# A later offer for the products of a recurrence: one constant in a planner that orders a whole kernel

## The chip, the core and the metric

The kernel runs on one core of a Trainium2 chip. The core has a matrix engine (TensorE, PE in the profile, with its weight loads shown apart as PEld), three engines for element work (VectorE or DVE, ScalarE or ACT, GpSimd or POOL), an engine that issues most transfers (SyncE, SP), and 16 DMA engines. Each engine works off its own queue in order. The metric is the device time of one launch in microseconds; less is better.

## The reference

One layer of a streaming encoder trunk works on 2048 prompt frames and 32 sample frames of width 1024. One input projection feeds two branches; branch A is attention in a band of chunks, branch B a gated delta rule with 8 heads of 64 in chunks of 64 frames. Both are gated, projected, merged, projected once more, added to the residual and normalised. The change lies in the delta rule's scan over the chunks:

```
def block(s, z):              # s: state (heads, 64, 64), one step per chunk
    r  = v  - k_decayed @ s           # what the state already explains
    vn = solve(r)                     # the chunk's triangular system
    o  = q_decayed @ s + qk @ vn      # the chunk's output
    s  = decay * s + k_rest.T @ vn    # the state for the next chunk
    return s, o
```

Each step needs the one before: three products and three element steps follow one another for 16 chunks per half of the prompt, for each pair of heads.

## The kernel before

The program is written by generators (streams) which a planner, `Flow`, resumes from a heap in the order of a modelled clock. What a stream emits between two yields is appended to the engines' queues, so the planner's clock sets the order in which each engine gets its work; on the chip nothing but queue order and data then decides when it runs. A bare `yield` puts the stream back at its own clock, plus `HOP_SAME` = 0.12 us if its last instruction was VectorE's; that addition moves only the key in the heap. A yielded float raises the stream's clock itself. `spend` books an instruction: it starts at the stream's clock plus a hop (`HOP_PE` = 0.1 for TensorE when the stream's last instruction was on another engine, `HOP` = 0.2 for the others) or when the modelled engine is free.

All engine instructions are recorded by one helper, so they carry line 267 in the profile (268 after the change, which adds a line above), and transfers carry 290 or 301.

The stages: the prompt is handled in two halves. In each, the input projection (`multiply`, tile `pj`, one matmul per yield, 512 or 272 columns wide, `hi`/`lo` and `whi`/`wlo` being the two parts of the split operands) runs beside the preparation and the recurrence of the delta rule (phase B, the recurrence at about 190 to 450 us and 910 to 1240 us) and then beside attention (phase A). In the second half's phase A the gated outputs of finished blocks already go through the branch projections (`early`, tiles `b<-ghi,whi`, `b<-glo,whi`), from about 1300 us on. The merge follows, from about 1709 us: for each block of 256 frames the merged activations (`mh`, their low part `ml`; `ms` for the sample rows) are multiplied with the output weights (`wohi`, `wolo`, `woh`, `wol`) into PSUM banks `a`, `a`, `a`, `c`, or by turns `pj`, `pj`, `b`, `b` once the early branch products are over. `finish` adds the result to the residual row `xt` (scaled before by rows `l0g`, `l0b` on GpSimd and VectorE), normalises and stores it.

The recurrence is `chain`, shown below. Tile names: `x` holds its three products (`x<-state,k_bd`, `x<-r,u_bd`, `x<-vn,kd_bd`), `o` its outputs, `r`, `vn` and `state` are VectorE's results. Two chains are open at a time (two banks `x`), and each takes a block of 8 chunks for a pair of heads; with the sample block there are 132 steps in all, hence 396 places where a product of TensorE follows VectorE. A small stream, `outputs`, emits the products into `o`.

Of the kernel before, what the change touches and what calls it, by code (L numbers as in the profile page):

```python
# [58 lines left out]
ORDER += [(NP - 1, 3)]  # L59
MARGIN = 1.6  # L60
SLACK = 2.5
LEAD = 5.0
ZERO = 1.2
BLOCKS = [
# [211 lines left out]
def trunk(ctx: ExitStack, tc: tile.TileContext, x_p, x_s, cache_k, cache_v, st_conv, st_gdn,  # L276
# [4 lines left out]
    flow = Flow()  # L281
# [6 lines left out]
    def dma(dst, src, eng=nc.sync):  # L288

        eng.dma_start(dst, src)  # L290
        size = 2 if dst.dtype == F16 else 4
        n = size
        for k in dst.shape:
            n *= k

        n = max(n, n // (size * dst.shape[-1]) * 768)
        return flow.transfer("SP" if eng is nc.sync else "S", n)

    def turn(dst, src):
# [5 lines left out]
        flow.busy["SP"] = max(flow.busy.get("SP", 0.0), flow.cur.clock + 0.2) + 0.8  # L305
        return flow.transfer("SP", n * 1.5) + SLACK

# [338 lines left out]
    def load_rows(w, k, to, ready):  # L646
# [4 lines left out]
        for c in range(2):  # L651
            hi, lo = to(c)
            flow.start(split(hi, lo, wr[:, c * 512:(c + 1) * 512], both[c], V if k % 2 else G, t + SLACK, ready(c)))
        yield
# [26 lines left out]
    def divide():  # L681

        while True:
# [7 lines left out]
            sc = w_scale[:, job.wid:job.wid + 1]  # L691
            yield t + (SLACK if len(started) > 4 else 0.0)
            started.append(job)
# [88 lines left out]
    def split(hi, lo, wr, give, eng, t, m):  # L782
        yield t
        S.copy(out=hi, in_=wr)
        yield
        eng.tensor_tensor(out=lo, in0=wr, in1=hi.bitcast(F32), op=ALU.subtract)
        if give:
            give()
        m.done()
# [50 lines left out]
    def phase_b(half):  # L840
# [535 lines left out]
        def outputs(m, x, os_, vc=None, end=None):  # L1376


            PE.matmul(os_, m, x, start=vc is None, stop=vc is not None)
            yield  # L1380
            if vc is not None:
                S.copy(out=vc, in_=os_)
                if end:
                    end.done()

        def chain(some):
            for k in some:
                yield k.ready
                xn = yield from x_banks.take()
                sc, v_t = k.sc, k.v_t  # L1390
                xs, ys, ds_ = (xb[xn][:, i * HD:(i + 1) * HD] for i in range(3))
                os_ = ob_[xn][:, 0:HD]
                for c in range(k.nch):
                    st = k.state[c]
                    vc = v_t[:, c if k.p is None else c % 4 * 2 + c // 4, :]
                    PE.matmul(xs, k.kb[:, c, :], st, start=True, stop=True)
                    yield
                    r = bp.tile([P, HD], F32, tag=f"r{xn}", bufs=2, name="r")
                    V.scalar_tensor_tensor(out=r[:], in0=xs, scalar=k.negc[:, c:c + 1], in1=vc, op0=ALU.mult, op1=ALU.add)
                    yield  # L1400
                    PE.matmul(ys, k.ub[:, c, :], r[:], start=True, stop=True)
                    flow.start(outputs(k.qb[:, c, :], st, os_))
                    yield
                    vn = bp.tile([P, HD], F32, tag=f"vn{xn}", bufs=2, name="vn")
                    V.tensor_scalar(out=vn[:], in0=ys, scalar1=sc[:, 1, c:c + 1], scalar2=None, op0=ALU.mult)
                    yield
                    PE.matmul(ds_, k.kdb[:, c, :], vn[:], start=True, stop=True)
                    flow.start(outputs(k.qkb[:, c, :], vn[:], os_, vc, k.out if c == k.nch - 1 else None))
                    V.scalar_tensor_tensor(out=st, in0=st, scalar=sc[:, 3, c:c + 1], in1=ds_, op0=ALU.mult, op1=ALU.add)
                    yield  # L1410
                yield k.out
                x_banks.back(xn)
                par_slots.back(k.par)
                side_slots.back(k.sn)
                u_slots.back(k.un)
                flow.start(tail(k))
# [87 lines left out]
        for some in blocks + ([[sample]] if last else []):  # L1504
            flow.start(chain(some))
# [3 lines left out]
    def phase_a(half):  # L1509
# [424 lines left out]
        def leave_pair(k, t, gt, place):  # L1934
# [4 lines left out]
            cs = slice(gt * P, (gt + 2) * P)  # L1939
            at = dma(ga[:].rearrange("p i n -> p (i n)"), za_dram[k.p][:, cs]) + SLACK  # L1940
            yield at - LEAD / 4
            yield bank["b"]
# [19 lines left out]
        def sample(k):  # L1962
# [12 lines left out]
            kc_t, vc_t = cached  # L1975
            yield at + SLACK
            yield bank["b"]
# [132 lines left out]
    def last_weights():  # L2110
# [6 lines left out]
        def load(k, c, half):  # L2117
            cs = slice(c * 512, (c + 1) * 512)
            t = dma(half, w_out[k * P:(k + 1) * P, cs])
            flow.start(split(wo[0][k][:, cs], wo[1][k][:, cs], half, None, V if k % 2 else G, t, w_ready["o", k, c]))  # L2120
            yield t - LEAD

        def row(name, src):
# [3 lines left out]
            if name[0:2] == "l0":  # L2127
                flow.start(scale(rowv[name][:], t, name == "l0b"))
            yield t - LEAD

        def scale(r, t, last):
            yield t
            S.activation(out=r, in_=r, func=AF.Copy, scale=ALPHA)
            if last:
                rows_ready.done()
# [90 lines left out]
    def early():  # L2226
        while True:
# [12 lines left out]
            for f in range(KD):  # L2240
# [12 lines left out]
                def evac(f=f, sg=sg, slots=slots, ps=ps, t=t, c0=c0, n=n, what=what, br=br):  # L2253
                    yield t + SLACK
                    V.scalar_tensor_tensor(out=sg[:, 0:n], in0=sg[:, 0:n], scalar=1.0, in1=ps[:, 0:n],
                                           op0=ALU.add, op1=ALU.mult)
                    bank["b"].give()
                    yield
                    at = dma(sig_dram[br][f][:, c0:c0 + n], sg[:, 0:n])
                    for b, _, _ in what:  # L2260
                        early_done[br, b, f].done()
                    yield at
                    slots.give()
# [278 lines left out]
```

## Time and profile before

| what | value |
|---|---|
| median of three runs | 1983.99 us |
| the runs | 1983.57, 1987.36, 1983.99 us |
| the profiled execution | 1980.36 us |
| its span in the profile | 1978.6 us |
| granted TensorE clock, mean over the span | 0.988 |
| TensorE busy | 1894.8 us, 14513 matmuls |
| VectorE busy | 1421.8 us, 4458 instructions |
| ScalarE busy | 993.2 us |
| GpSimd busy | 814.7 us |

The profile is one execution, with the begin and the duration of every instruction, and for the idle time of an engine the instruction that ended it. The group lines read: engine, operation, output tile and input tiles, shapes, count, then busy time in us, mean duration in ns, and the engine's idle time just before these instructions with what ended it. Timeline rows begin with the start and the duration in us, and have the idle time before them and its end in brackets.

### The profile page before, as it was taken

How to read it: one execution, taken by the hardware profiler on the slowest of the kernel's cores; microseconds unless marked ns; L12 is line 12 of the kernel's file. 1: busy time of each engine (PE TensorE's matmuls, PEld its weight loads, DVE VectorE, ACT ScalarE, POOL GpSimd, SP SyncE). 2: the span in 40 equal slices, each digit the busy share in tenths (PEclk: the TensorE clock that was granted, in tenths of full speed). 3: DMA queues.
4: the chain of work that ended last, by engine and by line, in shares of the span. 5: the costliest groups of instructions: out<-in, count | busy, mean ns of one | idle time of the engine just before them, and what ended most of it. 6: DMA issues, size and time to landing. Idle time of an engine off the chain costs nothing.

```text
span 1978.6 us, 41065 instructions
## 1 busy us (share of the span) xinstructions
PE 1894.8 (96%) x14513; PEld 1338.2 (68%) x14513; DVE 1421.8 (72%) x4458; ACT 993.2 (50%) x2022; POOL 814.7 (41%) x1139
## 2 busy tenths in 40 slices
PE   8999999999999999999999999999999999989996
PEld 5455666676455556666776777678877668878874
DVE  7779989873378768579989986356466665585886
ACT  6665545444586777664544533445355774310110
POOL 7344334433344444343333432423122331363695
PEclk9999999999999999999999999999999999999998
DMA  4224242333378786223142243578878798975542
GB/s 139 68 83 125 65 108 70 84 92 108 115 159 197 188 179 156 71 79 89 52 118 68 68 112 83 139 212 192 227 173 199 168 215 177 310 272 191 167 152 83
DMA packets 382806, 274.62 MB, mean 139 GB/s; under 512 B 248322, under 2 KB 319342, under 8 KB 382600
## 3 DMA queue, kind: packets, MB, share of 16 engines
q1 hardware_dynamic: 382600, 272.00, 51.3%
q8 instruction: 114, 1.87, 0.4%
q14 instruction: 92, 0.75, 0.1%
HBM read 157.15 MB, written 71.76 MB: 116 GB/s over the span
## 4 chain that ended last, share of the span: by engine, by line
PE 64%; DVE 20%; issue 5%; ACT 4%; DMA 4%; POOL 3%; SPq 1%; POOLq 0%; DVEq 0%; ACTq 0%
PE pj L267 34%; PE b L267 15%; PE a L267 7%; PE c L267 4%; PE x L267 3%; DVE acc L267 3%; DVE sys_t L267 2%; DVE sys_u L267 2%; PE o L267 2%; DVE kd_bd L267 1%; POOL wlo L267 1%; SPq L290 1%; DVE xt L267 1%; DVE q_bd L267 1%; DMA sf<-sig 1%
## 5 line engine op out<-in xcount | busy, mean ns | idle before, releaser
L267 PE MATMUL pj<-hi,whi 128*128 128x512 f16 (+2 forms) x1992 | 642.3, 338 | 11.2 <-DVE zb L267 3.2
L267 PE MATMUL pj<-hi,wlo 128*128 128x512 f16 (+2 forms) x1952 | 633.8, 338 | 0.6 <-POOL wlo L267 0.5
L267 PEld LDWEIGHTS <-whi 128*128 128x128 f16 x3984 | 407.8, 104 | 227.3 <-issue 8.6
L267 POOL TENSOR_TENSOR wlo<-wraw,whi 128x256 f16<-128x256 f32 (+1 forms) x392 | 280.6, 738 | 460.9 <-ACT whi L267 380.5
L267 PE MATMUL pj<-lo,whi 128*128 128x512 f16 (+2 forms) x1992 | 452.5, 338 | 0.0
L267 PEld LDWEIGHTS <-wlo 128*128 128x128 f16 x1952 | 204.3, 105 | 115.2 <-issue 11.9
L267 ACT ACTIVATE sb<-sb,mx,unit 128x640 f32<-128x640 f32 (+4 forms) x128 | 108.6, 849 | 101.4 <-DVE mx L267 96.3
L267 POOL TENSOR_TENSOR pu<-sb,pu 128x640 f16<-128x640 f32 (+2 forms) x64 | 82.3, 1285 | 178.3 <-ACT pu L267 145.4
L267 ACT ACTIVATE wraw<-wraw,w_scale 128x1024 f32<-128x1024 f32 (+1 forms) x98 | 111.4, 1137 | 78.3 <-DVE w_scale L267 75.8
L267 PE MATMUL b<-ghi,whi 128*128 128x256 f32 (+1 forms) x512 | 138.7, 303 | 3.6 <-DVE cr L267 1.1
L267 ACT CAST whi<-wraw 128x512 f16<-128x512 f32 (+2 forms) x212 | 128.2, 611 | 27.5 <-PE pj L267 24.6
L267 PE MATMUL b<-ghi,wlo 128*128 128x256 f32 (+1 forms) x512 | 129.5, 284 | 0.0
L267 DVE TENSOR_TENSOR sys_u<-sys_u,sys_t 128x60 f32<-128x60 f32 (+24 forms) x527 | 124.6, 242 | 5.7
L267 DVE SCALAR_TENSOR_TENSOR acc<-raw,cwT,acc 128x512 f32<-128x512 f32 x144 | 112.7, 782 | 7.9 <-ACT acc L267 6.5
L267 ACT CAST mh<-sf 128x256 fp32r<-128x256 f32 x64 | 25.7, 406 | 178.8 <-PE c L267 74.8
L267 DVE TENSOR_TENSOR sys_t<-sys_u,sys_p 128x60 f32<-128x60 f32 (+21 forms) x459 | 109.8, 242 | 5.5
L267 PEld LDWEIGHTS b<-ghi,whi 128*128 128x128 f32 x512 | 97.3, 190 | 9.7 <-ACT ghi L267 1.5
L267 ACT COPY v_t<-o 128x64 f32<-128x64 f32 x132 | 27.7, 210 | 143.2 <-PE o L267 106.7
L267 PEld LDWEIGHTS b<-ghi,wlo 128*128 128x128 f32 x512 | 97.5, 190 | 1.5
L267 DVE CUSTOM_DVE_ANT_0 sb<-a,bias 128x320 f32<-128x320 f32 (+5 forms) x136 | 66.2, 497 | 45.0 <-PE a L267 42.4
L267 POOL TENSOR_TENSOR w_scale<-w_scale,mhalf 128x1 f32<-128x1 f32 x49 | 32.2, 657 | 157.3 <-DVE w_scale L267 113.8
L267 ACT ACTIVATE sig<-pj,w_half 128x512 f32<-128x512 f32 (+2 forms) x84 | 49.3, 587 | 77.0 <-PE pj L267 71.6
(377 smaller groups left out, 4097.7 us busy)
## 6 DMA issues: line engine op xcount, KB each, us to landing
wraw<-in_w_in SPq DMA_DIRECT2D x192, 256.0 KB
sf<-sig SPq DMA_DIRECT2D x112, 128.0 KB
sig<-sig SPq DMA_DIRECT2D x44, 256.0 KB
sg<-sig SPq DMA_DIRECT2D x37, 256.0 KB
sig<-sg SPq DMA_DIRECT2D x37, 256.0 KB
sys_p<-sol_p SPq DMA_DIRECT2D x68, 128.0 KB
x<-in_x_p SPq DMA_DIRECT2D x16, 512.0 KB
xt<-in_x_p SPq DMA_DIRECT2D x16, 512.0 KB
```

What stands on the lines that cost most here:

```text
L267: r = f(*a, **k)
L290: eng.dma_start(dst, src)
```

## The change

Each of the chain's three yields that follow a VectorE instruction now yields a time instead of nothing: the stream's clock plus 0.15 us. Before, the stream came back at a key 0.12 us later with its clock unmoved; now key and clock are both 0.15 us later. The instructions themselves are the same.

```
+CHAIN = 0.15
...
                     V.scalar_tensor_tensor(out=r[:], in0=xs, scalar=k.negc[:, c:c + 1], in1=vc, op0=ALU.mult, op1=ALU.add)
-                    yield
+                    yield flow.cur.clock + CHAIN
                     PE.matmul(ys, k.ub[:, c, :], r[:], start=True, stop=True)
...
                     V.tensor_scalar(out=vn[:], in0=ys, scalar1=sc[:, 1, c:c + 1], scalar2=None, op0=ALU.mult)
-                    yield
+                    yield flow.cur.clock + CHAIN
                     PE.matmul(ds_, k.kdb[:, c, :], vn[:], start=True, stop=True)
...
                     V.scalar_tensor_tensor(out=st, in0=st, scalar=sc[:, 3, c:c + 1], in1=ds_, op0=ALU.mult, op1=ALU.add)
-                    yield
+                    yield flow.cur.clock + CHAIN
```

The order of all engines is the same up to the first steps of the first recurrence, and differs in many small pieces from there to the end. Three places follow.

TensorE in the first recurrence of half 0, before: `pj` are projection products, `b<-ident` transposes, the number behind a name tells tiles of one name apart.

```order
L267 MATMUL pj<-lo_163,whi 128x512
L267 MATMUL x<-vn,kd_bd_746 128x64
L267 LDWEIGHTS whi
L267 MATMUL pj<-lo_163,whi 128x512
L267 MATMUL o<-vn,qk_bd_739 128x64
L267 LDWEIGHTS whi
L267 MATMUL pj<-lo_163,whi 128x512
L267 MATMUL b<-ident,v_1845 128x128 x4
L267 LDWEIGHTS whi
L267 MATMUL pj<-lo_163,whi 128x512
L267 MATMUL x<-state,k_bd_735 128x64
```

The same place on TensorE after the change:

```order
L268 MATMUL pj<-lo_163,whi 128x512
L268 LDWEIGHTS whi
L268 MATMUL pj<-lo_163,whi 128x512
L268 MATMUL x<-vn,kd_bd_746 128x64
L268 MATMUL b<-ident,v_1845 128x128 x4
L268 LDWEIGHTS whi
L268 MATMUL pj<-lo_163,whi 128x512
L268 MATMUL o<-vn,qk_bd_739 128x64
L268 MATMUL x<-state,k_bd_735 128x64
```

The product of `vn` has moved behind projection products, and the next step's product of `state` is left with one projection product less ahead of it.

TensorE at the end of the second half's recurrence, before: the last chain of a pair (`state`) and the sample block's (`state_s`) alternate.

```order
L267 MATMUL x<-vn,kd_bd_9735 128x64
L267 LDWEIGHTS whi
L267 MATMUL pj<-hi_9067,whi 128x512
L267 MATMUL o<-vn,qk_bd_9726 128x64
L267 LDWEIGHTS wlo
L267 MATMUL pj<-hi_9067,wlo 128x512
L267 MATMUL x<-state_s,k_bd_9722 128x64
L267 LDWEIGHTS whi
L267 MATMUL pj<-hi_9067,whi 128x512
L267 MATMUL x<-r,u_bd_9737 128x64
```

The end of the second half's recurrence on TensorE after the change:

```order
L268 MATMUL x<-vn,kd_bd_9737 128x64
L268 LDWEIGHTS wlo
L268 MATMUL pj<-hi_9383,wlo 128x272
L268 MATMUL o<-vn,qk_bd_9728 128x64
L268 LDWEIGHTS whi
L268 MATMUL pj<-hi_9383,whi 128x272
L268 LDWEIGHTS wlo
L268 MATMUL pj<-hi_9383,wlo 128x272
L268 LDWEIGHTS whi
L268 MATMUL pj<-lo_9384,whi 128x272
```

The `state` chain now ends after the sample block's, alone, and between its products stand 272-wide instead of 512-wide projection products.

GpSimd at the last block of the merge, before: `xt<-xt,l0g` and `xt<-xt,l0b` scale the residual rows, `ml` and `ms` are low parts, `m` belongs to the normalisation.

```order
L267 TENSOR_TENSOR m_23935<-m_23935,mhalf 128x1
L267 TENSOR_TENSOR m_23949<-m_23949,mhalf 128x1
L267 TENSOR_TENSOR ml_21963<-sf,mh_21955 128x256
L267 TENSOR_TENSOR xt<-xt,l0g 128x256 x4
L267 TENSOR_TENSOR ms<-sf,ms 128x32
L267 TENSOR_TENSOR xt<-xt,l0g 32x256 x4
L267 TENSOR_TENSOR xt<-xt,l0b 128x256 x4
```

GpSimd at the same place after the change:

```order
L268 TENSOR_TENSOR m_23940<-m_23940,mhalf 128x1
L268 TENSOR_TENSOR ml_22048<-sf,mh_22040 128x256
L268 TENSOR_TENSOR xt<-xt,l0g 128x256 x4
L268 TENSOR_TENSOR xt<-xt,l0g 32x256 x4
L268 TENSOR_TENSOR ms<-sf,ms 128x32
L268 TENSOR_TENSOR m_23955<-m_23955,mhalf 128x1
L268 TENSOR_TENSOR xt<-xt,l0b 128x256 x4
```

The first `ms` has moved behind the sample row's scaling, and one `m` behind both. The sample rows' products, into bank `b` before, go into bank `a`, since the early branch products are over one block sooner in the planner's time.

More of the change, by code (lines that the diff above doesn't have):

```diff
@@ L61 @@
 SLACK = 2.5
+CHAIN = 0.15
 LEAD = 5.0
@@ L1399, in chain @@
                     V.scalar_tensor_tensor(out=r[:], in0=xs, scalar=k.negc[:, c:c + 1], in1=vc, op0=ALU.mult, op1=ALU.add)
-                    yield
+                    yield flow.cur.clock + CHAIN
                     PE.matmul(ys, k.ub[:, c, :], r[:], start=True, stop=True)
@@ L1405, in chain @@
                     V.tensor_scalar(out=vn[:], in0=ys, scalar1=sc[:, 1, c:c + 1], scalar2=None, op0=ALU.mult)
-                    yield
+                    yield flow.cur.clock + CHAIN
                     PE.matmul(ds_, k.kdb[:, c, :], vn[:], start=True, stop=True)
@@ L1409, in chain @@
                     V.scalar_tensor_tensor(out=st, in0=st, scalar=sc[:, 3, c:c + 1], in1=ds_, op0=ALU.mult, op1=ALU.add)
-                    yield
+                    yield flow.cur.clock + CHAIN
                 yield k.out
```

## The prediction

> **What bounds the kernel now.** I read the page first: the busy times, the slices of VectorE in tenths, and the shares of the chain that ended last.
>
> ```profile
> span 1978.6 us, 41065 instructions
> PE 1894.8 (96%) x14513; PEld 1338.2 (68%) x14513; DVE 1421.8 (72%) x4458; ACT 993.2 (50%) x2022; POOL 814.7 (41%) x1139
> DVE  7779989873378768579989986356466665585886
> PE 64%; DVE 20%; issue 5%; ACT 4%; DMA 4%; POOL 3%; SPq 1%; POOLq 0%; DVEq 0%; ACTq 0%
> ```
>
> TensorE is busy for 96% of the span, and 64% of the chain that ended last is TensorE's. Its products are the same before and after, so the change can only move the 1978.6 - 1894.8 = 83.8 us in which it stands, and what it runs at half clock. VectorE is at nine tenths only in slices 4 to 8 and 19 to 24, the two recurrences. I then asked for the busy times by stage; the columns are the stretch, its length, the busy time of PE, PEld, DVE, ACT and POOL, the granted clock, the DMA share and GB/s.
>
> ```profile
> 190.00:450.00 260.00, 251.40 (x2010) 175.26 (x2007) 225.08 (x895) 129.75 (x278) 100.06 (x167) 0.99 0.33 88
> 910.00:1240.00 330.00, 316.36 (x2845) 240.55 (x2845) 284.51 (x1103) 154.13 (x356) 116.74 (x206) 0.99 0.32 85
> 1690.00:1770.00 80.00, 72.33 (x484) 65.49 (x484) 56.23 (x92) 20.70 (x45) 39.93 (x44) 0.97 0.92 314
> 1900.00:1980.00 80.00, 60.67 (x246) 45.48 (x244) 54.41 (x82) 5.02 (x18) 54.59 (x60) 0.87 0.30 102
> ```
>
> The two recurrences hold 8.60 + 13.64 = 22.2 us of TensorE's idle time. The opening of the merge (1690 to 1770) holds 7.7 and the last 80 us hold 19.3, at a granted clock of 0.97 and 0.87. Then I read who waits for whom in the recurrence: the list of waits (us, times, longest) and the groups.
>
> ```profile
> PEld x L267 <- DVE r L267: 23.7, 62, 1.6
> PEld x L267 <- DVE vn L267: 22.8, 54, 1.3
> PEld x L267 <- DVE state L267: 14.5, 46, 1.3
> L267 PE MATMUL x<-vn,kd_bd 128*128 128x64 f32 x264 | 50.7, 274 | 6.4 <-DVE vn L267 6.0
> L267 PE MATMUL x<-state,k_bd 128*128 128x64 f32 x256 | 48.9, 272 | 2.1 <-DVE state L267 1.5
> L267 PE MATMUL x<-r,u_bd 128*128 128x64 f32 x264 | 48.8, 267 | 7.1 <-DVE r L267 4.5 <-DVE sys_u L267 1.8 <-DVE sys_t L267 0.2
> ```
>
> The chain has 132 steps of three links, 396 in all. The loads of the three products wait 61.0 us for VectorE in 162 waits. That is the most the change could win in its own place: a waiting load partly lies under products still in the array, whose own idle time is 6.4 + 2.1 + 7.1 = 15.6 us, the other bound. So a little time is there, in many small pieces.
>
> **The change, part by part.** It adds no engine instruction. In the planner, a chain's next product is offered 0.15 us later, and the stream's own clock moves with it (before, only the key in the heap moved, by 0.12). What follows is another order, from the first recurrence to the end.
>
> *The links.* A product offered later helps only if other products get ahead of it. What such a cushion is worth, by start to start:
>
> ```profile
> 561.23 0.38 PE L267 MATMUL pj<-hi,wlo 128*128 128x512 f16 x1
> 561.45 0.38 PE L267 MATMUL pj<-hi,whi 128*128 128x512 f16 x1
> 1682.65 0.28 PE L267 MATMUL pj<-hi,wlo 128*128 128x272 f16 x1
> 1682.76 0.28 PE L267 MATMUL pj<-hi,whi 128*128 128x272 f16 x1
> ```
>
> A 512-wide projection product buys 0.22 us and a 272-wide one 0.11. Counted in the two orders, the products that stand between a chain's product and its next one are: 512-wide 873 before and 872 after, 272-wide 537 and 506, others 454 and 460. That is 31 x 0.11 - 0.22 = about 3.4 us less cushion over all links, 0.01 us each: with both chains and the projections competing for one queue, what is put before one link is taken from another. By kind, the work between r's product and vn's rises by 0.05 us, between state's and r's it falls by 0.03, between vn's and state's by 0.02. I take 0. The ends: all of the 61.0 us of load waits gone cannot be, since 15.6 us of it is plain idle and 22.2 us all the idle time there is; a gain of half the 22.2, 11 us, is the lower end, and +3.4 (every lost cushion becomes a wait) the upper.
>
> *The ends of the recurrences.* In half 0 the last chain ends 8 us of TensorE work earlier in the order, and the streams are in step again before phase A; nothing waits for it. In half 1 the last pair's chain ends 5.4 us later and the transposes that close the phase 2.5 us later, now against 272-wide projections. Behind them the opening of phase A is a chain that the page's critical path enters here:
>
> ```profile
> 1237.46 6.94 PE pj L267 x53
> 1252.58 5.61 issue
> 1280.22 5.03 DMA kst<-part
> 1290.74 1.91 PE pj L267 x15
> ```
>
> Between 1285 and 1298 TensorE stands 1.33 + 0.75 + 0.58 + 1.08 = 3.7 us in its four largest gaps:
>
> ```profile
> 1287.05 0.28 PE L267 MATMUL pj<-hi,whi 128*128 128x272 f16 x1 [1.33 <-ACT part L267]
> 1290.74 0.29 PE L267 MATMUL pj<-hi,whi 128*128 128x272 f16 x1 [0.75 <-DVE ql L267]
> 1295.58 0.60 PE L267 MATMUL b<-ident,carry_s 128*3 128x128 f32 x4 [0.58 <-ACT v_s L267]
> 1297.26 0.39 PE L267 MATMUL b<-ghi,whi 128*128 128x256 f32 x1 [1.08 <-DVE cr L267]
> ```
>
> Half of the 2.5 us is covered by projections that are left over: +1.2, ends 0 and +5.4.
>
> *The merge's opening.* The early branch products move up to 22 us earlier, the last projections of half 1 about 24 us later, and the first merge block 20 us later. The third product of the merge's second block waits for a bank that VectorE empties only when the residual row is there:
>
> ```profile
> 1760.82 0.40 PE L267 MATMUL a<-wohi,mh 128*128 128x512 f32 x1
> 1761.06 0.39 PE L267 MATMUL a<-wolo,mh 128*128 128x512 f32 x1
> 1767.89 0.80 PE L267 MATMUL a<-wohi,mh 128*128 128x512 f32 x1 [5.97 <-DVE xt L267]
> 1768.49 0.63 PE L267 MATMUL a<-wolo,mh 128*128 128x512 f32 x1
> 1768.91 0.63 PE L267 MATMUL c<-wohi,mh 128*128 128x512 f32 x1
> 1772.30 0.39 PE L267 MATMUL a<-wohi,mh 128*128 128x512 f32 x1
> ```
>
> Products start every 0.23 us ahead of the wait and every 0.43 us behind it, for the ten products up to 1772.30: the wait costs 5.97 and the half clock 4.41 - 10 x 0.23 = 2.1 more, 8.1 in all. The TensorE work between the last projection and this product is 69 us before and 63 after, so 6 us of cover are gone if the row comes at the same distance from the last projection. On SyncE the row's first operand, l0g, is issued 37 places later (910 for 873), behind loads and stores of the branch products, which come earlier with them. But DMA was at a share of 0.92 here (the stretch from 1690), and with the branch products earlier its load is spread too. I take 0, between -8.1 (the row is there) and +6 + 2 = +8. The Trainium skill, "TensorE: Matmul & The Clock Gate", Part 1, states that the array falls to half clock after an idle window of about 3.4 us and comes back after a like window of work. The trace agrees (5.97 us idle, then 0.43 us for 4.4 us). By that rule a wait that stayed under the window would cost no clock, and one that is lengthened from 5.97 costs no second loss: by it the upper end would be +6, not +8.
>
> *The tail.* The sample rows' products (32 of 0.23 us) wait for their low parts, which GpSimd makes:
>
> ```profile
> 1927.90 0.40 PE L267 MATMUL b<-wolo,ms 128*64 128x512 f32 x1
> 1934.24 0.69 PE L267 MATMUL b<-wohi,ms 128*64 128x512 f32 x1 [5.95 <-POOL ms L267]
> 1940.69 0.69 PE L267 MATMUL b<-woh,ms 128*64 128x512 f32 x1 [3.63 <-DVE ms L267]
> 1946.55 0.39 PE L267 MATMUL b<-woh,ms 128*64 128x512 f32 x1
> 1915.02 9.04 POOL L267 TENSOR_TENSOR xt<-xt,l0g 128x256 f32<-128x256 f32 x4 [2.08 <-DVE xt L267]
> 1924.23 2.80 POOL L267 TENSOR_TENSOR xt<-xt,l0g 32x256 f32<-32x256 f32 x4
> 1933.95 0.24 POOL L267 TENSOR_TENSOR ms<-sf,ms 128x32 fp32r<-128x32 f32 x1
> 1837.18 2.96 POOL L267 TENSOR_TENSOR xt<-xt,l0g 128x256 f32<-128x256 f32 x4 [3.17 <-DVE xt L267]
> ```
>
> From 1928.13 to 1946.55 twenty products take 18.4 us where 20 x 0.23 = 4.6 would do: 13.8 us lost, 9.6 of it waiting, the rest at half clock. GpSimd's queue sets this: four steps took 9.04 us where the same four took 2.96 earlier. After the change the first ms stands behind the 2.80 us step instead of ahead of it, the second where it was, and the bank is a, not b. The wait that decides is for the second, so I take 0; the ends are -13.8 (the 9.04 shrinks to 2.96 and the wait goes) and +2.8. The Trainium skill, "SBUF — State Buffer", Who interferes with whom, says that VectorE with two SBUF inputs holds a port that GpSimd reads through. The trace's 9.04 against 2.96 for one shape fits it, with no proof; by it the tail turns on which VectorE steps fall beside those four, which no order tells.
>
> **Sum.** 0 + 1.2 + 0 + 0 = +1.2 on this profiled execution of 1980.36 us (its span of 1978.6 and 1.8 around it): 1981.6. The runs' median, 1983.99, is 3.6 above that execution, so I forecast a median of 1985.2. A change under 0.2%, 4 us, can hardly be told from none in this kernel (its three runs span 1983.57 to 1987.36); so this is no change.
>
> **The rivals.**
> - *The order now fits the hand-over, and waits in the recurrence shrink.* For it: 162 of 396 links are seen to wait. Against it: no more cushion stands there. If half of the 22.2 us idle goes: 1984.0 - 11 = 1973; a third gives 1977.
> - *The tail's wait falls away.* The row to win is 13.8 us: 1984.0 + 1.2 - 13.8 = 1971. For it: it hangs on a 9.04 us accident of GpSimd; against it: GpSimd was busy for 54.59 of the last 80 us, and the merge's blocks now follow one another more tightly, which leaves it less slack.
> - *Slower: the merge opens with the row late.* 6 us less cover turns into a wait of 12 us instead of 5.97, plus 2 us of clock, with the 1.2: 1984.0 + 9.2 = 1993. It decides once the row lands no sooner after the last projection than before. With the row 3 us sooner it is 1988, the edge of no change.
> - *The change doesn't do what it says:* the cushions stay as counted and the re-shuffling cancels: 1984.
>
> **How the numbers follow.** Forecast (1981 to 1989) 0.40, of it 0.24 within 0.2%, 0.12 slower, 0.04 faster; shrunken waits 0.17 (0.15 faster, 0.02 same); tail gone 0.10 (0.09 and 0.01); late row 0.23 (0.21 slower, 0.02 same); no effect 0.10 (0.08 same, 0.01 each side). Sums: faster 0.29, same 0.37, slower 0.34. The range: the tail's 1971 and the late row's 1993 are single prices, and either may come with the phase end's bounds; from 1972 to 1997 about 2 in 10 is left out, half at each end. The forecast's own range is 1981 to 1989.
>
> **What would show it.** Links: the three load waits again near 61 us in about 160 waits; the first rival needs them under 45. Phase end: the gaps at 1285 to 1298 longer by about 1 us. Merge: the third product of the second block waiting 6 us again; 10 or more is the slower rival, none a gain of 8. Tail: the wait for ms near 9.6 us, the last 80 us again at a clock near 0.87. The forecast is wrong if one wait of over 3 us comes or goes where TensorE has no other work in its queue, since two such places hold 22 us.

## The result, and the profile after

| kernel | median of the runs | ratio to the kernel before (95% interval) |
|---|---|---|
| before | 1985.49 us (six runs) | |
| the change, 0.15 us | 1998.0 us (six runs, 1994.83 to 2005.55) | 1.0070 (1.0047 to 1.0093) |

The change costs 0.7%, some 12.5 us, and the time lies 1 us above the range of the prediction. The profiled execution after took 1994.83 us, that of before 1980.36; both lie 3 to 5 us below their medians, so their difference, 14.5 us in the spans, can be read for places but not to the microsecond.

The page of the changed kernel, the lines that answer to those of before, and its busy times by stage (stretch, length, busy PE, PEld, DVE, ACT, POOL, clock, DMA share, GB/s):

```profile
span 1993.1 us, 41094 instructions
PE 1898.2 (95%) x14513; PEld 1342.0 (67%) x14513; DVE 1426.8 (72%) x4458; ACT 993.4 (50%) x2022; POOL 818.9 (41%) x1139
190.00:450.00 260.00, 248.12 (x2041) 173.93 (x2040) 224.40 (x889) 130.13 (x280) 104.10 (x172) 0.99 0.33 89
910.00:1240.00 330.00, 317.07 (x2834) 240.97 (x2832) 284.84 (x1093) 152.86 (x353) 118.17 (x206) 0.99 0.32 87
1300.00:1690.00 390.00, 377.13 (x3394) 291.64 (x3395) 216.49 (x681) 207.74 (x424) 109.96 (x118) 0.99 0.81 195
1690.00:1770.00 80.00, 78.77 (x664) 71.29 (x663) 38.80 (x78) 21.30 (x49) 19.34 (x20) 1.00 0.84 257
1770.00:1900.00 130.00, 118.00 (x572) 99.95 (x572) 100.00 (x159) 20.81 (x45) 82.53 (x93) 0.95 0.58 195
```

The same stretch of phase A before the change, which the prediction did not look at:

```profile
1300.00:1690.00 390.00, 385.86 (x3567) 298.98 (x3567) 220.94 (x697) 209.60 (x427) 108.35 (x118) 1.00 0.81 196
```

TensorE's idle time in the recurrences is 11.9 + 12.9 us, 2.6 more than before. In phase A (1300 to 1690) it rises from 4.1 to 12.9 us. In the merge's opening the old 7.7 us fall to 1.2, and 12.0 us appear behind 1770, where 0.9 stood. Up to 1240 us all stretches together have 1.2 us more idle time; from 1240 to 1690 it is 8.5 more; from there to the end 1.5 more. TensorE's busy time grows by 3.4 us with the same products, since its clock was at half speed for longer (mean granted clock 0.983, before 0.988).

The waits of the changed kernel: of the chain's loads, then of TensorE, the longest two (us in all, times, longest).

```profile
PEld x L268 <- DVE r L268: 23.5, 63, 1.2
PEld x L268 <- DVE vn L268: 22.0, 53, 1.5
PEld x L268 <- DVE state L268: 16.8, 48, 1.0
PE b L268 <- DVE sl L268: 12.0, 1, 12.0
PE a L268 <- POOL ms L268: 5.4, 1, 5.4
```

The load waits are 62.3 us in 164 waits, 61.0 in 162 before: at its own place the change did nothing. The loss has one large piece, a single wait of 12 us for bank `b`, released by VectorE's `sl`, the evacuation of an early branch product. VectorE's timeline ahead of that release, and what TensorE and GpSimd do there (start and duration in us):

```profile
1786.49 1.43 DVE L268 TENSOR_TENSOR xt<-xt,l0g 128x256 f32<-128x256 f32 x4
1787.84 1.96 DVE L268 TENSOR_SCALAR xt<-xt,mv 128x1024 f32<-128x1024 f32 x2
1789.71 3.02 DVE L268 TENSOR_TENSOR xt<-xt,l0b 128x256 f32<-128x256 f32 x4
1792.66 3.53 DVE L268 TENSOR_TENSOR xt<-xt,l0g 128x256 f32<-128x256 f32 x4
1799.46 2.47 DVE L268 TENSOR_TENSOR xt<-xt,l0b 128x256 f32<-128x256 f32 x4
1802.58 0.44 DVE L268 SCALAR_TENSOR_TENSOR sl<-sl,b 128x288 f32<-128x288 f32 x1
1803.08 0.61 PE L268 MATMUL b<-ghi,whi 128*128 128x288 f32 x1 [12.01 <-DVE sl L268]
1803.48 0.44 PE L268 MATMUL b<-ghi,wlo 128*128 128x288 f32 x1
1807.32 0.29 PE L268 MATMUL b<-ghi,wlo 128*128 128x288 f32 x1
1807.45 0.29 PE L268 MATMUL b<-ghi,whi 128*128 128x288 f32 x1
1789.87 3.44 POOL L268 TENSOR_TENSOR xt<-xt,l0g 128x256 f32<-128x256 f32 x4 [0.63 <-DVE xt L268]
1793.28 3.49 POOL L268 TENSOR_TENSOR xt<-xt,l0b 128x256 f32<-128x256 f32 x4
```

The rows are picked; in the full timeline VectorE never stands still from 1785 to 1803. The four groups of `l0g` and `l0b`, which scale two residual row tiles, are 10.4 us of these 17, and the 0.44 us step for which TensorE waits comes behind them. The four `l0g` steps take 1.43 us while GpSimd is idle and 3.53 us while GpSimd does the same work. Behind the wait the products start every 0.24 us instead of every 0.13, for 17 products: 4.24 - 17 x 0.13 = 2.0 us more. So this place costs 14.0 us now; the old one, for bank `a`, cost 8.1. There too the evacuation for which TensorE waited stood behind row scaling, in a stretch (1748 to 1768) in which VectorE had no idle time:

```profile
1753.30 3.60 DVE L267 TENSOR_TENSOR xt<-xt,l0g 128x256 f32<-128x256 f32 x4
1761.31 3.54 DVE L267 TENSOR_TENSOR xt<-xt,l0b 128x256 f32<-128x256 f32 x4
1767.17 0.67 DVE L267 SCALAR_TENSOR_TENSOR xt<-a,xt 128x512 f32<-128x512 f32 x1
```

In phase A the loss is in several waits of 1.2 to 2.5 us, three of them (5.4 us together) for a projection bank. One of these, ScalarE first and TensorE below:

```profile
1544.08 1.32 ACT L268 CAST ghi<-glo 128x256 fp32r<-128x256 f32 x4 [5.42 <-DMA glo<-g]
1545.83 1.05 ACT L268 ACTIVATE za<-pj,w_half 128x512 f32<-128x512 f32 x2
1547.28 0.28 PE L268 MATMUL pj<-hi,whi 128*128 128x272 f16 x1 [2.51 <-DVE za L268]
```

The cast `ghi` of an early branch waits 5.42 us for its transfer. The bank is emptied by a `za` step on ScalarE and one on VectorE, and ScalarE's stands behind the cast in its queue.

Waits as short as this can cost clock as well. Behind a wait of 2.50 us, at the opening of phase A, products that had started every 0.22 us started every 0.42 us:

```profile
1283.84 0.38 PE L268 MATMUL pj<-hi,whi 128*128 128x512 f16 x1 [2.50 <-ACT part L268]
1284.06 0.38 PE L268 MATMUL pj<-hi,wlo 128*128 128x512 f16 x1
1285.63 0.63 PE L268 MATMUL pj<-hi,wlo 128*128 128x512 f16 x1
1286.05 0.63 PE L268 MATMUL pj<-hi,whi 128*128 128x512 f16 x1
```

The granted clock was 0.50 for 3.41 us here (1285.06 to 1288.47), and as long behind the 2.51 us above (1547.88 to 1551.29). From 1240 to 1690 its mean is 0.98 where it was 1.00, so this stretch costs more than its idle time. Not every short wait does this: behind one of 3.07 us, at 914.58, the clock stayed at 1.00.

### The profile page after: what moved, and what is told of

Same layout as the page of the kernel before. It is cut to its first block, busy times and chain, and to the rows that moved or that the text cites. A ratio compares the mean times of both kernels' runs of the same rounds, so it can differ in the third digit from the quotient of the medians.

```text
span 1993.1 us, 41094 instructions
## 1 busy us (share of the span) xinstructions
PE 1898.2 (95%) x14513; PEld 1342.0 (67%) x14513; DVE 1426.8 (72%) x4458; ACT 993.4 (50%) x2022; POOL 818.9 (41%) x1139
## 5 line engine op out<-in xcount | busy, mean ns | idle before, releaser
L268 PEld LDWEIGHTS <-wlo 128*128 128x128 f16 x1952 | 204.8, 105 | 118.6 <-issue 14.5
L268 PE MATMUL b<-ghi,whi 128*128 128x256 f32 (+1 forms) x512 | 141.9, 309 | 14.5 <-DVE sl L268 12.0
L268 DVE TENSOR_TENSOR sys_u<-sys_u,sys_t 128x28 f32<-128x28 f32 (+22 forms) x527 | 124.2, 243 | 5.3
L268 DVE TENSOR_TENSOR sys_t<-sys_u,sys_p 128x54 f32<-128x54 f32 (+20 forms) x459 | 110.6, 245 | 5.2
L268 DVE SCALAR_TENSOR_TENSOR sg<-sg,b 128x512 f32<-128x512 f32 (+2 forms) x56 | 34.4, 615 | 86.1 <-PE b L268 75.7
```

The lines of the kernel that those rows point to most:

```text
L268: r = f(*a, **k)
```

## The experiments

The orders that the planner gives tell how to ask. They differ inside the recurrences for every delay, but behind them they fall into few classes: one is the old kernel's queue, product for product, another the changed kernel's. So the delay and the queue behind it can be varied apart. Ratios are to the kernel before as it ran beside each experiment (medians 1985.2 to 1986.9 us), with 95% intervals.

**One half at a time.**

```
-                    yield flow.cur.clock + CHAIN
+                    yield None if half else flow.cur.clock + CHAIN     # first half only
+                    yield flow.cur.clock + CHAIN if half else None     # second half only
```

> The delay of 0.15 us in the first half's recurrence alone. In the order that the planner gives, TensorE's queue is the changed kernel's up to the end of the first half, and the old kernel's, product for product, from about 943 us on. Theory A (the delay is worth nothing at its own place; the time is lost where the re-shuffled order behind the recurrences meets late VectorE work in the phase A opening, phase A's end and the merge): 1985 to 1989 against 1985.5, that is the 2 us by which the changed kernel's trace lags at 900 us, with the old waits of about 6 us in the merge's opening and 6 + 4 in the tail. Theory B (each delayed link costs, since the planner's clock of the chain runs ahead of the chip's): half of the loss, 1991 to 1992.

> The delay in the second half's recurrence alone. The order is the old kernel's up to about 943 us and the changed kernel's from there to the end. Theory A: nearly the whole loss, 1995 to 1999, with the wait of 12 us before b<-ghi,whi in the merge's opening and no 6 us wait of a<-wohi,mh. Theory B: half of the loss, 1991 to 1992.

Measured: first half alone 1987.31 us, 1.0013 (1.0003 to 1.0023); second half alone 2000.14 us, 1.0075 (1.0057 to 1.0092), with the 12.0 us wait for `sl`. As theory A has it: the order from 943 us on gives the whole loss, and the first half's delay costs 2 us (0.03 to 0.23%). What the second half's recurrence itself does is not parted here from the order behind it; the next runs do that.

**Another delay, the old queue behind it.** `CHAIN = 0.16` and `CHAIN = 0.5`. From about 1431 us on their queue is the old one.

> The delay is 0.16 us instead of 0.15, at all places. The order within the recurrences is another one, but from about 1431 us to the end TensorE's queue is the old kernel's, product for product. Theory A: the waits of phase A's end and of the merge are the old ones again, about 1985 to 1990 (what the opening of phase A loses, up to 5 us, may stay). Theory B: as the changed kernel, 1998 to 1999.

> The delay is 0.5 us at all places, over three times the change's; from about 1431 us to the end TensorE's queue is again the old kernel's. Theory A: 1985 to 1992, as with 0.16, unless the recurrence itself gets longer; the loads of the chain's products then wait less, under 50 us instead of 62, since more work stands ahead of them, and the idle time saved is under 10 us. Theory B: the loss grows with the delay, 2010 or more.

Measured: 0.16 gives 1985.05 us, 1.0000 (0.9988 to 1.0012); 0.5 gives 1986.54 us, 1.0004 (0.9994 to 1.0014). A hundredth of a microsecond more than the change, and the loss is gone; three times the delay, and it isn't there either. Theory B (each delayed link costs) falls. The load waits at 0.5 are 48.2 us, under the 50 expected, without a shorter time; the waits are read again under larger delays.

**One link in three, the changed queue behind it.** The delay after `r` alone, the other two yields bare.

> Only the first of the three yields (after r) has the delay of 0.15 us, a third of the change. The order within the recurrences is another one, but from about 1261 us to the end TensorE's queue is the changed kernel's, product for product. Theory A (the loss lies in the waits that the order behind the recurrences makes): 1995 to 2000 against 1985.5, with the 12 us wait of b<-ghi,whi. Theory B (each delayed link costs): a third of 12.5 us, 1989 to 1990.

Measured: 2001.32 us, 1.0084 (1.0067 to 1.0101), with a 12.0 us wait for `sl`. A third of the delays gives the whole loss.

**The key without the clock.**

```
+            elif isinstance(what, tuple):
+                self.push(s, what[0])
...
-                    yield flow.cur.clock + CHAIN
+                    yield (CHAIN,)
```

> The key alone is moved by 0.15 us (0.12 before); the stream's clock stays. The queue is neither the old nor the changed one behind the recurrences (it shares the changed kernel's from about 1825 us on), and is the same as with a delay of 0.12 us on key and clock. Theory B (the moved clock costs): 1984 to 1988. Theory A gives no number of its own beforehand, only that the difference to 1985.5 is found again as single waits of over 1 us behind 1240 us, and not in the recurrences, whose load waits stay at 52 to 66 us.

Measured: 1999.68 us, 1.0071 (1.0054 to 1.0088): theory B is out by 12 us again. The load waits are 59.7 us. This third queue loses at other steps of the same kind, TensorE's longest waits behind 1690 us being:

```profile
PE a L270 <- POOL ms L270: 8.4, 3, 5.2
PE b L270 <- ACT ghi L270: 7.5, 1, 7.5
PE a L270 <- DVE ms L270: 3.9, 1, 3.9
PE b L270 <- DVE glo L270: 3.2, 1, 3.2
```

**The 12 us wait itself.** The changed kernel, with VectorE scaling one residual row tile, and none, instead of two; GpSimd does the rest.

```
-        eng = V if gt < 2 else G
+        eng = V if gt < 1 else G        # "rows 1";  "rows 0": eng = G
```

> The changed kernel, but only the first residual row tile is scaled (l0g, l0b) on VectorE and the second on GpSimd, where both were VectorE's. TensorE's queue is the changed kernel's up to the products before the 12 us wait. Theory A1 (the wait is VectorE's queue: the evacuation of bank b stands behind the scaling of two row tiles, whose steps take over twice as long beside GpSimd's): 6 us of scaling fall away ahead of it, so the wait is 12 - 6 = 6 us or less and the time 1988 to 1993. Theory A2 (the evacuation waits for its own operand from memory, the queue only looks guilty): the wait stays 12 us and the time 1996 to 2000. Theory A3: GpSimd gets the rows ready so late that the bank a waits instead, and the time stays within 3 us of the changed kernel's although the wait at b goes.

> The changed kernel with no residual row tile scaled on VectorE; GpSimd scales all. A1: some 10 us less VectorE work stands ahead of the evacuation of bank b, the wait falls under 3 us, the time is 1984 to 1990. A2: wait of 12 us, 1996 to 2000. A3: the wait at b goes and one of 6 us or more for bank a (behind the rows) comes, 1992 to 2000.

Measured: rows 1 gives 1997.43 us, 1.0063 (1.0046 to 1.0081), rows 0 gives 1990.98 us, 1.0032 (1.0016 to 1.0047). The first waits of each, rows 1 above, rows 0 below:

```profile
PE b L268 <- DVE sl L268: 8.6, 1, 8.6
PE a L268 <- POOL ms L268: 7.0, 1, 7.0
```

```profile
PE a L268 <- POOL ms L268: 8.4, 1, 8.4
PE b L268 <- DVE sl L268: 4.6, 2, 3.7
```

The wait goes from 12.0 over 8.6 to 3.7 as the row scaling leaves VectorE's queue, so it is the queue (A1) and not the evacuation's own operand (A2). The times alone would not tell: that of rows 1 is hardly shorter and lies in the range that A2 gave, and that of rows 0 lies 1 us above A1's. The sizes were too hopeful: 6 us of work taken away shortened the wait by 3.4, and in both the tail's wait for `ms` behind GpSimd grows (5.4, 7.0, 8.4) and takes part of it back, a form of A3. With the wait at 3.7 us 0.3% of loss remain. The trace of rows 0 still has 17.4 us of idle time from 1240 to 1690 us, where the kernel before has 8.2; but it is one execution, the fastest of twelve (1986.02 us). Rows 0 was not run on the kernel before, so it is not shown how much of the 7 us it would bring there.

**The same edit on the kernel before.**

> The kernel before with the same edit: only the first residual row tile on VectorE. If the old wait of 6 us (third product of the second merge block, bank a) is the same VectorE queue, A1 lets it fall to under 2 us, which with the half clock behind it is worth up to 8: 1977 to 1982. A3: GpSimd takes three row tiles at a time, the second tile's row is ready later than before and bank a waits longer: 1985 to 1992.

Measured: 1978.52 us, 0.9962 (0.9948 to 0.9977), with the old wait for bank `a` at 2.5 us instead of 6.0:

```profile
PE b L267 <- POOL ms L267: 4.4, 1, 4.4
PE b L267 <- POOL glo L267: 2.8, 3, 1.3
PE a L267 <- DVE xt L267: 2.5, 1, 2.5
```

The wait for bank `a` falls by 3.5 us, less than expected (under 2 us left), and 2.5 more for `glo` come elsewhere in the merge. Most of the gain lies where it was not looked for, in the tail: the waits for `ms`, 5.95 and 3.63 us in the kernel before, are one of 4.4 now. So VectorE's queue at the merge's opening holds up TensorE in both kernels, and the change moved what it hits; but the 6.7 us of this run are not the price of that place. Two further edits, `V.tensor_tensor` for all `ms`, and that with no yield between the second row tile's two scalings:

```
-                eng.tensor_tensor(out=ms[:, f, DEC:], ...
+                V.tensor_tensor(out=ms[:, f, DEC:], ...
...
-            yield                # x_load, between l0g and l0b
+            if gt != 1:
+                yield
```

> The kernel before with the second residual row tile scaled on GpSimd (as in the run that gave 1978.5) and, new, all low parts of the sample rows (ms) made on VectorE, where every second one was GpSimd's and waited behind its row scaling for 4.4 us in the last block. If that queue alone set the tail: 4.4 us and some half clock less, 1972 to 1976. If VectorE, with its own steps of up to 5.2 us there, takes its place: 1976 to 1981.

> As the run before, and the second row tile's two scalings emitted together, so that GpSimd does not put the third and fourth tile's first scaling (10.8 us for twelve steps) ahead of the second tile's last one. If the wait of 2.5 us for bank a in the merge's second block comes from that order: about 3 us less than the run before, 1970 to 1975; if the row was not late for it: no change from it.

Measured: 1978.35 us, 0.9959 (0.9944 to 0.9974), and 1979.59 us, 0.9968 (0.9958 to 0.9979). Neither brings anything over 1978.5. The wait for `ms` is 4.4 us again, now on VectorE; and where the wait for bank `a` falls to 0.5 us, one of 5.6 for `glo` comes.

**Larger delays.** `CHAIN = 0.3`, with the changed kernel's queue behind the recurrences.

> The delay is 0.3 us, twice the change's, at all places. The order within the recurrences is another one; from about 1261 us to the end TensorE's queue is the changed kernel's, product for product. Theory A: as the changed kernel, 1995 to 2001 against 1985.5, with its 12 us wait of b<-ghi,whi. Theory B: twice the loss, 2010 or more. With the delays of 0.16 and 0.5, whose queues end as the old one, A says that the time follows the queue behind the recurrence and not the delay.

Measured: 1982.87 us, 0.9982 (0.9971 to 0.9994). Both theories miss, A by 12 us. The wait for `sl` is there, at 12.4 us, but the chain's loads wait less:

```profile
PEld x L268 <- DVE vn L268: 18.7, 40, 1.7
PEld x L268 <- DVE r L268: 13.7, 30, 1.0
PEld x L268 <- DVE state L268: 11.7, 24, 1.0
```

That is 44.1 us in 94 waits where 0.15 has 62.3 in 164. The queues of the two are the same from about 1261 us on. In the two profiles the first product of that stretch starts at 1253.6 us with 0.15 and at 1237.5 with 0.3, and what follows takes 739.5 and 743.5 us: the gain lies ahead of the shared queue, and the loss behind it is still there. The order shows why the links wait less. The table has the most frequent numbers of projection products between a chain's product and its next one, after `r`, `state` and `vn`, and the numbers of all that stand there, 512 and 272 wide, counted as in the prediction:

| delay | after r, state, vn | all, 512 and 272 wide | load waits, us (times) |
|---|---|---|---|
| before (key 0.12) | 2, 3, 2 | 873, 537 | 61.0 (162) |
| 0.15 | 2, 3, 2 | 872, 506 | 62.3 (164) |
| 0.16 | 2, 3, 2 | 894, 543 | 54.2 (145) |
| 0.24 | 2, 3, 2 | 926, 597 | 55.2 (123) |
| 0.3 | 3, 4, 3 | 1015, 680 | 44.1 (94) |
| 0.32 | 3, 4, 3 | 992, 693 | 45.6 (90) |
| 0.5 | 4, 5, 4 | 1201, 771 | 48.2 (90) |

The most frequent numbers move only in whole products, and 0.03 us more on the key moves none of them. This made a new theory, C, and its rival D, tested at 0.24 and 0.32 (old queue from 1316 and 1431 us on) and at 0.34 in the first half alone (old queue from 943 us on).

> The delay is 0.24 us. Between the chain's products stand most often 2, 3 and 2 projection products (after r, after state, after vn), as with 0.12 and 0.15; from about 1316 us to the end TensorE's queue is the old kernel's. Theory C (two things add up: the recurrence gets shorter only from the delay at which one more projection product of 0.22 us fits into each link, and the queue behind it is either the old one or the changed one, 12 us worse): no more product fits yet, the queue is the old one, so 1982 to 1989 against 1985.5, with the chain's load waits at 52 to 66 us. Theory D (the delay itself shortens the recurrence, in proportion: 0.3 gave about 14 us): 0.24 gives about 10, so 1974 to 1978.

> The delay is 0.32 us: 3, 4 and 3 projection products stand most often between the chain's products, and from about 1431 us to the end TensorE's queue is the old kernel's. Theory C: the recurrence's gain of the run with 0.3 (8 us in the first half, 6 in the second, of which an opening of phase A may take back 5) without the changed kernel's queue behind it: 1971 to 1978, load waits under 48 us. Theory A alone (the delay is worth nothing at its own place): 1983 to 1989.

> A delay of 0.34 us in the first half's recurrence alone, where it puts 3, 4 and 3 products into the links; from about 943 us on TensorE's queue is the old kernel's. Theory C: the first half's gain of 5 to 8 us and nothing else: 1977 to 1981. Theory A alone: 1984 to 1988, as with 0.15 in the first half.

Measured: 0.24 gives 1979.48 us, 0.9970 (0.9959 to 0.9982), between the two theories. 0.32 gives 1976.30 us, 0.9958 (0.9941 to 0.9975), within C and against A. The first half alone gives 1987.42 us, 1.0007 (0.9995 to 1.0018), against C. Its load waits up to 465 us fell from 29.6 us in 76 to 25.0 in 49, but its attention stage, from 590 to 670 us, waits where before only 3.2 us idle stood:

```profile
PE c L268 <- DVE ob L268: 5.6, 3, 3.7
PE b L268 <- ACT whi L268: 2.2, 1, 2.2
```

So theory C, in range once in its three tests, is not shown. At 0.24 the most frequent numbers are the old ones, as it says, but more products stand in the links in all and the load waits fall; and at 0.5, with the old queue behind it and load waits as short as at 0.32, the time is not shorter. What stands is that a longer delay shortens the waits of the links; whether the time keeps that is not told by the delay. The opening of the second phase A takes some back too: at 0.32 a projection bank waits 4.5 us for ScalarE's `part`, where the longest wait for it was 1.3 before.

**The best of both.** `CHAIN = 0.32` and rows 1 together.

> The delay of 0.32 us, and the second residual row tile scaled on GpSimd instead of VectorE, which alone brought 7 us. The two act at different places (recurrence, merge opening), so they add: 1964 to 1971 if theory C holds for 0.32, 1976 to 1981 if it doesn't. If the sum is short of the parts by 4 us or more, what one saves is waited for again by the other.

Measured: 1968.98 us, 0.9914 (0.9900 to 0.9928). The two parts, 0.42 and 0.38%, add up to 0.80; the sum is 0.86. This kernel is 0.86% faster than the one before, and some 29 us faster than the changed one.

## Why the prediction was wrong

The step that failed is the sum of +1.2 us. It put the merge's opening at 0, where the trace has +5.9, and it had no term for phase A, from 1300 us to the merge, where the trace has +8.7 us of idle time. The runs show that the order behind the recurrences makes this loss: it comes with the changed queue and goes with the old one, at nearly the same delay.

- *The links, taken as 0:* right. The three load waits were forecast near 61 us in about 160 waits; they are 62.3 in 164. The forecast counted the cushion in the order; the runs at 0.3 and 0.32 showed what it looks like when it does change. Its sum of what was lost has a wrong sign in it: both counts fall, so 31 x 0.11 + 0.22 = 3.6 us, not 3.4; the upper end of this term moves by that 0.2 and nothing else.
- *The ends of the recurrences, +1.2 (0 to +5.4):* the gaps at the opening of phase A were right in kind (2.5 us for ScalarE's `part`, 0.8, 1.2 and 0.5 behind it), but the step stopped at 1300 us. The missing term is phase A, 1300 to 1690: +8.7 us of TensorE's idle time. The early branch products had been seen to move up to 22 us earlier; they were read as relief for the merge, and what they do to ScalarE's and VectorE's queues on the way, in a stretch that had only 4.1 us idle, was not asked. One of the waits there was followed to such a product (the 5.42 us at `ghi`); for the others this is not shown.
- *The merge's opening, taken as 0 (-8.1 to +8):* this term was mis-sized. The wait that was watched went (-8.1), and one of 14.0 with its half clock came 35 us later for another bank: +5.9 in sum. That this lies inside the bounds is luck, since they were worked out for the old wait alone. The slower rival (chance 0.23) had the sign and the stage, and its 12 us for the wait came out by luck as well: it was to be the old wait, behind a row late from memory. VectorE's queue, full for 17 us, is what held the new one, as rows 1 and rows 0 showed; the old one too ended behind row scaling in that queue, not at a late transfer. The sign that the prediction named for being wrong came twice: a wait of 6.0 us went and one of 12.0 came.
- *The tail, taken as 0 (-13.8 to +2.8):* a little better than that, 5.4 + 0.9 us of waiting for 9.6.
- *The sum:* two terms of re-shuffled order, +8.5 between 1240 and 1690 and +5.9 in the merge, were netted at +1.2. With all pieces bounded singly, nothing said that they would cancel.
- The Trainium skill's "TensorE: Matmul & The Clock Gate", Part 1, states half clock after an idle window of about 3.4 us and full clock after a like window of work. The latter fits the two long waits in kind: 4.4 us of slow products behind 5.97 us of waiting, 4.2 behind 12.01. The former does not cover this trace: the clock was at half behind waits of 2.50 and 2.51 us too, so the prediction's reading, that a wait under the window costs no clock, was wrong here.
- The Trainium skill's "SBUF — State Buffer", Who interferes with whom, was cited for the tail only. Its place was the merge's opening: there VectorE's steps with two SBUF inputs took 3.53 us beside GpSimd's and 1.43 alone, which agrees with the rule.

What stays open: TensorE's idle time from 1240 to 1690 us follows the queue (7.1 to 8.5 us in the seven runs whose queue is the old one from 1316 us or earlier, and at 0.16; 15.4 to 17.4 in the six with the changed one; 11.7 to 14.4 in between, at 0.5 and 0.32, where the old queue begins at 1431), but no run took one of these waits away by itself. Why 0.5 gains nothing from its shorter load waits is open. How the gain of 0.24, 0.3 and 0.32 divides between the two halves is open too: single executions of one and the same order differ by some 6 us between 890 and 1200 us (the run with the delay in the first half only, against the kernel before).

## What to carry to other kernels

A constant that moves keys in a planner's heap re-writes the queues behind it, and much of the time is decided there: before trusting or blaming the constant, look for two values of it that end in the same queue, and for two queues under nearly one value. Count in the order what the constant admits, all of it and not the most frequent number alone. Look for a short evacuation behind a burst of other work in an in-order queue: moving one row tile's scaling off VectorE brought 0.38% here (most of it in the tail, where it was not looked for), about as much as the best of the delays (0.42%), and the two added up.

## What the runs showed of the hardware

Four VectorE steps of 128x256 with both operands in SBUF took 1.43 us alone and 3.0 to 3.6 us beside the same work on GpSimd. TensorE's clock was at half for 3.41 us behind waits of 2.50 and 2.51 us. Executions of one program differed by up to 10 us in this kernel (1979.5 to 1989.8 in 29 executions of the kernel before), half a per cent, and the changed kernel's ran from 1994.8 us at a mean granted clock of 0.983 to 2005.6 at 0.977; a single profile is not enough to place 3 us.
